# A hybrid decoder stack on one Trainium2 core: attention's value sums completed in memory, rotary latent queries laid out by matrix products

## The chip, the cores and the metric

The kernel runs on one core of one Trainium2 chip. The metric is the device time of one execution in microseconds (us). The engines are named as in the profile: PE (TensorE matmul), PEld (TensorE weight load), DVE (VectorE), ACT (ScalarE), POOL (GpSimd) and SP (SyncE, which issues the DMAs here).

## The reference, cut to what matters

Two post-norm decoder layers on 1024 tokens of width 1024, in float32. In each layer one input projection feeds four mixers side by side, whose outputs are joined and projected; then come a layer norm, a SwiGLU network of inner width 2816, and another layer norm.

```python
y_a = _gmlp_mixer(...)      # chunked spatial gating
y_b = _mla_mixer(...)       # latent attention, 4 heads, 64 plain + 32 rotary columns
y_c = _dilated_mixer(...)   # three dilated windows, 4 heads of 64
y_d = _mlstm_mixer(...)     # chunkwise mLSTM
y = jnp.concatenate([y_a, y_b, y_c, y_d], axis=-1) @ w_out[l]
x = _layer_norm(DEEPNORM_ALPHA * x + y, ln1_g[l], ln1_b[l])
h = (jax.nn.silu(x @ w_gate[l]) * (x @ w_up[l])) @ w_down[l]
x = _layer_norm(DEEPNORM_ALPHA * x + h, ln2_g[l], ln2_b[l])

# latent attention
q = (_rms_norm(c_q) @ w_uq).reshape(..., GROUP_HEADS, 64 + 32)
q = jnp.concatenate([q[..., :64], _rope(q[..., 64:], pos)], -1)
kv = (_rms_norm(c_kv) @ w_ukv).reshape(..., GROUP_HEADS, 64 + 64)
k = jnp.concatenate([k_nope, k_rope broadcast over heads], -1)
o = causal softmax(q k^T / sqrt(96)) v
```

## The kernel before, in words

**Precision.** A float32 product is made of products in the type fp32r. Each operand is split into a high part, a copy in fp32r, and a low part, the difference (`split`, L140 to L146: the copy on ACT, the subtraction on DVE or POOL). `mms` (L121 to L124) issues the chains of matmuls, so most matmuls of the profile bear line L124.

**Order of a layer.** `build` runs the mixers' projections (`mix_a`, `mix_d`, `z_b`, `z_c`), then `attention`, `out_proj`, `ffn1`, `ffn2`. Instructions are placed by a scheduling layer; inside attention the order on PE is instead the order of the program (`manual_schedule`, `MAN`), while the queues of DVE, ACT, POOL and SP are still set by the scheduler.

**Attention** (`attn`, L792). There are four groups of two heads: groups 0 and 1 are the dilated mixer, groups 2 and 3 the latent one. A group has 16 rows, a row being 128 queries of one head; the query blocks come in pairs (`jp` 0 to 3), in the order 0 and 3, then 1 and 2. For a row, `scores` (L798) multiplies queries and keys into PSUM in chunks of 512 keys: two matmuls a chunk, three in the latent groups, where the third takes the rotary part (`QR` and `R`). DVE adds the mask and takes the maximum (L816), ACT makes the exponential (L820), POOL divides by the sum (L823). `turn` transposes the row (tile `pt`, L840) and splits the result into `PH` and `PL`. Two rows later `values` (L849) multiplies by the values (`pv`, L861). Scores run three rows ahead. Between rows PE takes jobs from a list (`fill`), which prepare the next group's operands, so that a job's matmuls stand in PE's queue between those of two rows.

**Sum halves of the values.** The value tile holds the high part in columns 0 to 63 and the low part in 64 to 127, so `pv` has two halves over partitions that must be added. Two ACT copies (L873, L874) bring them to the tile `tmp`, POOL adds them (L875). For groups 0 and 1 the sum goes to memory (`ys`, L877), for 2 and 3 into the tiles `Yb`. Four of the eight value blocks of group 0 have no low part ("full", L871).

**Queries.** `put_q` (L784) makes for each head `q1` (the high part in both halves of the partitions: two ACT copies, L787 and L789) and `q2` (the low part on DVE, L788; the other half set to zero by POOL, L790).

**Rotary part of the latent queries.** For each quarter of the tokens, `rot` multiplies (`prb`), rotates on DVE, and writes each head's 32 columns four times side by side (`qr`, two DVE instructions of 128x512, L1033). `turn` of `b_vqr_jobs` transposes these (`ptr`, eight of 128x128, L1044) and makes `QR`: ACT copies all (L1047), DVE puts the low part over half of it (L1048). In the list of jobs it is `rot`, `vals`, `turn` for each quarter.

**Output projection** (`out_proj`). `prep_w` loads and splits the weights, `ysplit(h)` (L1183) loads the mixers' outputs for one half of the tokens into tiles `yr` and splits them into `yT`; both use the pool `r` of two buffers. Then `proj` multiplies (`po`), half by half.

Of the kernel before, what the change touches and what calls it, by code (L numbers as in the profile page):

```python
# [13 lines left out]
L = 2  # L14
# [4 lines left out]
NT = S // 128  # L19
# [39 lines left out]
class Net:  # L59
# [712 lines left out]
    def qk_tiles(self, pool, pool2=None):  # L772
        f = lambda n, p=pool: self.u(n, F32R, p)
        return [f("kst") for _ in range(2)], [f("q1") for _ in range(2)], [f("q2", p) for p in (pool2 or (pool, pool))]
# [8 lines left out]
    def put_q(self, pq, q1, q2, cols):  # L783
        nc = self.nc  # L784
        for hh in range(2):
            r, o = slice(64 * hh, 64 * hh + 64), slice(64 - 64 * hh, 128 - 64 * hh)
            nc.scalar.copy(q1[hh][r, cols], pq[r, :])  # L787
            nc.vector.tensor_sub(q2[hh][r, cols], pq[r, :], f32(q1[hh][r, cols]))  # L788
            nc.scalar.copy(q1[hh][o, cols], pq[r, :])  # L789
            nc.gpsimd.tensor_scalar(out=q2[hh][o, cols], in0=self.ident[o, 0:1].to_broadcast([64, 512]), scalar1=0.0, scalar2=None, op0=ALU.mult)  # L790

    def attn(self, groups):  # L792
# [57 lines left out]
        def values(n):  # L850
# [5 lines left out]
            pairs = PHL.pop((id(G), jp, hh))  # L856
            m = 64 if full else 128
            for b in range(nb):
                c0 = 128 if b == nb - 1 else 0
                for x, Pt in enumerate(pairs):  # L860
                    nc.tensor.matmul(pv[0:m, c0:256], lhsT=V[2][:, b, hh * 64:(hh + 1) * 64] if full else V[hh][:, b, :], rhs=Pt[b // 4][:, b % 4, c0:256],  # L861
                                     start=b == 0 and x == 0, stop=b == nb - 1 and x == len(pairs) - 1)
            tmp = self.t2("tmp", 512)
            y, spill = tmp[0:64, 0:256], None
            if "Y" in G:
                y = G["Y"][jp // 2][64 * hh:64 * hh + 64, (jp % 2) * 256:(jp % 2) * 256 + 256]
            else:
                l, g = G["spill"]
                spill = self.io["ys"][l, 2, jp // 2, 64 * hh:64 * hh + 64, g * 512 + (jp % 2) * 256:g * 512 + (jp % 2) * 256 + 256]
            if full:  # L870
                nc.scalar.copy(y, pv[0:64, 0:256])  # L871
            else:
# [105 lines left out]
    def b_vqr_jobs(self, ct, w, out):  # L978
# [4 lines left out]
        def rotk(half):  # L983
# [8 lines left out]
            for r in (slice(32, 64), slice(96, 128)):  # L992
                nc.vector.tensor_sub(R[r, cols], pt[r, :], f32(R[r, cols]))
        def start():
            out["V"] = [[self.u("V", F32R if i < 2 else F32, "A").rearrange("p (t n) -> p t n", t=NT) if (any(f) if i == 2 else not all(f)) else None
                         for i in range(3)] for f in FULL[2:]]
            out["QR"] = [[self.u("QR", F32R, "A").rearrange("p (h n) -> p h n", h=2) for _ in range(2)] for _ in range(2)]
        def vals(t2):
# [6 lines left out]
            pv = pv.rearrange("p (t n) -> p t n", t=2)  # L1005
            ts = slice(t2 * 2, t2 * 2 + 2)
            for g in range(2):
                if FULL[2 + g][t2]:
                    nc.scalar.copy(V[g][2][:, ts, :], pv[:, :, g * 128:(g + 1) * 128])
                if all(FULL[2 + g]):  # L1010
                    continue
                for hh in range(2):
                    self.split(V[g][hh][:, ts, 0:64], V[g][hh][:, ts, 64:128], pv[:, :, g * 128 + hh * 64:g * 128 + hh * 64 + 64])
        box = {}

        def rot(t2):
# [700 lines left out]
```

## Time and profile before

| | |
|---|---|
| three runs, median (lowest to highest) | 2463.27 us (2462.56 to 2467.29) |
| the profiled execution, its own time | 2466.75 us |
| its span, first to last instruction | 2465.0 us |
| busy: PE, PEld, DVE, ACT, POOL | 96%, 81%, 68%, 42%, 52% |
| mean granted clock of TensorE | 0.983 of full speed |
| attention of layer 0, of layer 1 (us from the span's start) | 283 to 460, 1514 to 1692 |

The busy shares are means over very different stages. The feed-forward networks hold more than half of the span, and there PE has no gaps to speak of; attention is the stage in which all engines work and PE waits. A wait is put down to the event that came last.

### The profile page before, as it was taken

To read this page: it belongs to the slowest core of one execution; us is meant where nothing else is said; L and a number is where in the kernel's file an instruction comes from. 1 tells how busy PE (TensorE), PEld (TensorE's weight loads), DVE (VectorE), ACT (ScalarE), POOL (GpSimd) and SP (SyncE) were. 2 spreads that over 40 slices of the span, in tenths; PEclk is the share of its full clock that TensorE was granted. 3 is DMA by queue.
4 is the path that set the end of the run, shared out by engine and by line. 5 is a ranking of instruction groups with operands and counts; after the bars stand their busy time and mean duration, and the time that the engine had idled before them with its cause. 6 is when DMAs were issued, how large, how long until landed. Compare 5 with 4: busy or idle time off the path is not lost.

```text
span 2465.0 us, 33578 instructions
## 1 busy us (share of the span) xinstructions
PE 2369.9 (96%) x11820; PEld 1992.5 (81%) x11820; DVE 1664.2 (68%) x2986; ACT 1035.7 (42%) x2102; POOL 1287.5 (52%) x1164
## 2 busy tenths in 40 slices
PE   9999878999999999999999999889999999999997
PEld 9889867787888888788797898778878888887886
DVE  7743687469665564789956436774696665647999
ACT  6322568524332323543333226695243323225442
POOL 2124536665555454776621245366655554547865
PEclk9999999999999999999999999899999999999999
DMA  4111001421332332643221110014213323326431
GB/s 166 53 34 48 18 9 57 172 93 52 129 111 82 118 104 102 257 164 123 99 66 52 35 48 18 8 57 171 94 52 129 111 85 117 108 101 253 166 120 68
DMA packets 83350, 237.37 MB, mean 96 GB/s; under 512 B 10912, under 2 KB 13280, under 8 KB 83184
## 3 DMA queue, kind: packets, MB, share of 16 engines
q1 hardware_dynamic: 83184, 235.24, 27.5%
q8 instruction: 94, 1.54, 0.3%
q14 instruction: 72, 0.59, 0.1%
HBM read 174.88 MB, written 60.33 MB: 95 GB/s over the span
## 4 chain that ended last, share of the span: by engine, by line
PE 79%; DVE 11%; ACT 5%; POOL 3%; issue 2%; DMA 0%; POOLq 0%; DVEq 0%; ACTq 0%; SPq 0%
PE gu L124 32%; PE dn L124 13%; PE po L124 6%; PE zc L124 5%; PE zvo L569 4%; PE zdq L521 3%; PE za L124 3%; PE zb L124 3%; PE sc L124 2%; PE pv L861 2%; DVE P L816 1%; PE pt L840 1%; ACT P L820 1%; DVE T L1347 1%; DVE PL L146 1%
## 5 line engine op out<-in xcount | busy, mean ns | idle before, releaser
L124 PE MATMUL gu<-T,fc 128*128 128x512 f32 x2640 | 631.0, 396 | 9.7 <-ACT fc L1265 8.0
L124 PEld LDWEIGHTS gu<-T,fc 128*128 128x128 f32 x2640 | 498.4, 189 | 130.2 <-ACT fc L1265 10.0
L1266 POOL TENSOR_TENSOR fc<-fw,fc 128x512 fp32r<-128x512 f32 x256 | 365.6, 1433 | 348.4 <-ACT fc L1265 344.1
L124 PE MATMUL dn<-dc,dc 128*128 128x512 f32 x1512 | 355.0, 397 | 4.8 <-DVE dc L1266 4.8
L124 PEld LDWEIGHTS dn<-dc,dc 128*128 128x128 f32 x1512 | 286.4, 190 | 73.1 <-DVE dc L1266 5.7
L1265 ACT CAST fc<-fw 128x512 fp32r<-128x512 f32 x256 | 156.9, 620 | 383.1 <-PE gu L124 211.3
L124 PE MATMUL gu<-B,fc 128*128 128x512 f32 x1056 | 258.9, 395 | 0.0
L146 POOL TENSOR_TENSOR dc<-hr,dc 128x512 fp32r<-128x512 f32 x126 | 195.9, 1570 | 85.8 <-ACT dc L143 75.1
L124 PEld LDWEIGHTS gu<-B,fc 128*128 128x128 f32 x1056 | 198.0, 188 | 46.9
L1396 DVE TENSOR_TENSOR Ra<-Ra,gu 128x512 f32<-128x512 f32 x172 | 117.7, 684 | 126.7 <-PE gu L124 111.5
L823 POOL TENSOR_SCALAR P<-P,rs 128x256 f32<-128x256 f32 (+7 forms) x128 | 99.1, 779 | 125.5 <-DVE rs L822 103.8
L124 PE MATMUL po<-wh,yT 128*128 128x512 f32 x512 | 162.1, 396 | 0.0
L124 PE MATMUL zc<-wh,xT 128*128 128x384 f32 x512 | 134.1, 339 | 0.0
L137 POOL TENSOR_TENSOR wl<-raw,wh 128x768 fp32r<-128x768 f32 (+2 forms) x40 | 81.9, 2052 | 85.5 <-ACT wh L132 84.9
L124 PE MATMUL sc<-kst,q 128*128 128x512 f32 (+3 forms) x384 | 111.8, 388 | 12.9 <-DVE mn L816 12.9
L840 PE MATMUL pt<-ident,P 128*128 128x128 f32 x576 | 93.3, 287 | 23.5 <-DVE PL L146 14.9
L124 PEld LDWEIGHTS po<-wh,yT 128*128 128x128 f32 x512 | 96.2, 188 | 22.2
L143 ACT CAST dc<-hr 128x512 fp32r<-128x512 f32 x126 | 77.6, 621 | 82.6 <-DMA hr<-hs 54.8
L1266 DVE TENSOR_TENSOR dc<-dr,dc 128x512 fp32r<-128x512 f32 x72 | 88.5, 1239 | 33.9 <-ACT dc L1265 33.7
L820 ACT ACTIVATE P<-P,mn 128x256 f32<-128x256 f32 (+7 forms) x128 | 99.5, 779 | 27.7 <-DVE mn L816 25.9
L146 DVE TENSOR_TENSOR PL<-pt,PH 128x512 fp32r<-128x512 f32 (+3 forms) x176 | 95.0, 557 | 20.5 <-ACT PH L143 19.3
L1266 POOL TENSOR_TENSOR fc<-s,fc 128x512 fp32r<-128x512 f32 x44 | 68.3, 1553 | 69.7 <-ACT fc L1265 26.2
(378 smaller groups left out, 5034.7 us busy)
## 6 DMA issues: line engine op xcount, KB each, us to landing
fw<-in_wGU SPq DMA_DIRECT2D x88, 512.0 KB, 4.8
hr<-hs SPq DMA_DIRECT2D x142, 256.0 KB, 2.9
dr<-in_wD SPq DMA_DIRECT2D x44, 512.0 KB, 6.2
hs<-Ra SPq DMA_DIRECT2D x40, 512.0 KB, 2.9
hs<-Rb SPq DMA_DIRECT2D x22, 512.0 KB, 5.5
raw<-in_wO SPq DMA_DIRECT2D x16, 512.0 KB, 3.8
x<-x SPq DMA_DIRECT2D x16, 512.0 KB, 2.6
raw<-in_wC SPq DMA_DIRECT2D x16, 384.0 KB, 3.1
```

Of the source, the lines that this page charges most:

```text
L124: self.nc.tensor.matmul(out, lhsT=a, rhs=b, start=first and j == 0, stop=last and j == n - 1)
L137: (eng or nc.gpsimd).tensor_sub(lo[:, :n], raw[:, :n], f32(hi[:, :n]))
L143: nc.scalar.copy(hi, src)
L146: (lo_eng or nc.vector).tensor_sub(lo, src, f32(hi))
L521: step(lambda: nc.tensor.matmul(pz, lhsT=a, rhs=b_, start=n == 0, stop=n == 23))
L569: nc.tensor.matmul(box["p"], lhsT=a, rhs=b_, start=j == 0, stop=j == 23)
L820: nc.scalar.activation(P[:, 0:nk], P[:, 0:nk], AF.Exp, scale=-1.0, bias=m, accum_out=rs[:, 0:1])
L823: nc.gpsimd.tensor_scalar(out=P[:, 0:nk], in0=P[:, 0:nk], scalar1=rs[:, 1:2], scalar2=1.0, op0=ALU.mult, op1=ALU.mult)
L840: nc.tensor.transpose(pt[:, b * 128:(b + 1) * 128], P[:, (b0 + b) * 128:(b0 + b + 1) * 128], self.ident)
L1265: nc.scalar.copy(dst[:, 0:512], src)
L1266: lo_eng.tensor_sub(dst[:, 512:1024], src, f32(dst[:, 0:512]))
L1396: tt = lambda o, a, b, op: v.tensor_tensor(out=o, in0=a, in1=b, op=op)
```

## The change

It has five parts, each made in both layers.

1. **Values.** In groups 0, 1 and 2 one ACT copy takes both halves of `pv` (128x256), and two DMAs of 64x256 write them to two parts of a new array `yp`; for the blocks without a low part, zeros are written from a constant. In group 3 ACT copies one half and DVE adds the other out of PSUM. `ysplit` loads both parts (two loads more for each half of the tokens) and DVE adds them (three adds of 128x512 for each half). `Yb` is one tile.
2. **Queries.** `q1`'s second half is copied by POOL from the first half, in place of ACT's copy from PSUM. `q2`'s zeros are written once for groups 0 and 1, and groups 2 and 3 use the same `q2` tiles again, so that no zeros are written for them.
3. **Rotary queries.** `rot` writes each head once (`qs`, 128x256). For each half of the tokens there are four transposes, one split into `qh` and `ql`, and for each head two matmuls of 512 columns (`pqr`) with a constant of ones and zeros (`selq`), which put copies and parts in their places; ACT copies the result to `QR`. `R`'s halves change to match.
4. **Values of the latent groups** are split by pairs of token blocks, all four heads at once (128x512).
5. The jobs' order changes with it, and `maskC` is loaded before the first group's preparation.

```diff
     def qk_tiles(self, pool, q2=None):
...
+        if q2 is None:
+            q2 = [f("q2") for _ in range(2)]
+            for hh in range(2):
+                o = slice(64 - 64 * hh, 128 - 64 * hh)
+                self.nc.gpsimd.tensor_scalar(out=q2[hh][o, :], in0=self.mask[o, :], scalar1=0.0, scalar2=None, op0=ALU.mult)
...
             nc.scalar.copy(q1[hh][r, cols], pq[r, :])
             nc.vector.tensor_sub(q2[hh][r, cols], pq[r, :], f32(q1[hh][r, cols]))
-            nc.scalar.copy(q1[hh][o, cols], pq[r, :])
-            nc.gpsimd.tensor_scalar(out=q2[hh][o, cols], in0=self.ident[o, 0:1].to_broadcast([64, 512]), scalar1=0.0, scalar2=None, op0=ALU.mult)
+            nc.gpsimd.tensor_copy(q1[hh][o, cols], f32(q1[hh][r, cols]))
...
-                nc.scalar.copy(tmp[0:64, 0:256], pv[0:64, 0:256])
-                nc.scalar.copy(tmp[0:64, 256:512], pv[64:128, 0:256])
-                nc.gpsimd.tensor_tensor(out=y, in0=tmp[0:64, 0:256], in1=tmp[0:64, 256:512], op=ALU.add)
-            if spill is not None:
-                nc.sync.dma_start(spill, y)
+                y = G["Y"][64 * hh:64 * hh + 64, jp * 256:(jp + 1) * 256]
...
+                    nc.scalar.copy(tmp[0:64, :], pv[0:64, 0:256])
+                    nc.vector.tensor_tensor(out=y, in0=tmp[0:64, :], in1=pv[64:128, 0:256], op=ALU.add)
+                return
+            nc.scalar.copy(tmp[0:m, :], pv[0:m, 0:256])
+            for part in range(2):
+                dst = G["spill"][part][64 * hh:64 * hh + 64, jp * 256:(jp + 1) * 256]
+                nc.sync.dma_start(dst, self.io["c_zero"][:, 0:256] if full and part else tmp[64 * part:64 * part + 64, :])
...
-            qrs = []
-            for j in range(2):
-                qr = self.t2("qr", 512).rearrange("p (h a n) -> p h a n", h=4, a=4)
-                nc.vector.tensor_tensor(out=qr, in0=a[:, j].unsqueeze(2).to_broadcast([128, 4, 4, 32]), in1=b[:, j].unsqueeze(2).to_broadcast([128, 4, 4, 32]), op=ALU.add)
...
+            nc.vector.tensor_tensor(out=qs, in0=a, in1=b, op=ALU.add)
+
+        def turn(half):
...
+            pt = self.psum("ptr", "t")
+            for j in range(4):
+                nc.tensor.transpose(pt[:, j * 128:(j + 1) * 128], box["qs"][:, j * 128:(j + 1) * 128], self.ident)
+            box["Q"] = self.t2("qh", dt=F32R), self.t2("ql", dt=F32R)
+            self.split(*box["Q"], pt)
+
+        def lay(half, h):
+
+            pq = self.psum("pqr", "mm")
+            self.mms(pq, [(box["sel"][:, (2 * h + e) * 128:(2 * h + e + 1) * 128], box["Q"][e]) for e in range(2)])
+            nc.scalar.copy(out["QR"][h // 2][half][:, h % 2, :], pq)
...
-        for t2 in range(4):
-            jobs += [f(rot, t2), f(vals, t2), f(turn, t2)]
-        jobs += [f(rotk, half) for half in range(2)]
+        for half in range(2):
+            jobs += [f(rot, 2 * half), f(vals, 2 * half), f(rot, 2 * half + 1), f(vals, 2 * half + 1), f(rotk, half), f(turn, half)]
+            jobs += [(lambda a, b: lambda: lay(a, b))(half, h) for h in range(4)]
...
+                    for f in range(2 if g == 2 else 1):
+                        raw = self.uw("yr", F32, "r")
...
+                        nc.vector.tensor_tensor(out=y[f], in0=y[f], in1=raw[:, 512:1024], op=ALU.add)
```

Three places show how instructions move. The first is PE in group 1 of layer 0, at the first rotary transposes (`ptr`). Before:

```order
L124 MATMUL pvb_3408<-wk_3321,kvT_2202 128x256
L840 MATMUL pt_3423<-ident,P_3259 128x128 x4
L124 MATMUL sc_3431<-kst_2936,q_448_2938 128x256
L124 MATMUL sc_3431<-kst_2936,q_450_2940 128x256
L1044 MATMUL ptr_3439<-ident,qr_3404 128x128
L1044 MATMUL ptr_3439<-ident,qr_3406 128x128
```

And now:

```order
L845 MATMUL pt_3459<-ident,P_3277 128x128 x2
L124 MATMUL sc_3466<-kst_2934,q_448_2936 128x512
L999 MATMUL ptb_3479<-ident,kr_1873 128x128 x4
L1043 MATMUL ptr_3490<-ident,qs_3400 128x128 x4
L124 MATMUL pqr_3499<-qh_3495,selq_3488 128x512
L124 MATMUL pqr_3499<-ql_3496,selq_3488 128x512
L872 MATMUL pv_3503<-PT_3300,zcv_2274 64x256 x3
```

The transposes now stand behind more work of the rows, and the first laying-out products (`pqr`) directly behind the transposes whose split they read.

The second is POOL at the change from group 1 to group 2 in layer 0 (`q_69*` and `q_7*` are the query tiles of groups 2 and 3, `P` the rows to divide). Before:

```order
L790 TENSOR_SCALAR q_690_3854<-ident 64x512 x2
L823 TENSOR_SCALAR P_3870<-P_3870,rs_3880 128x768
L823 TENSOR_SCALAR P_3910<-P_3910,rs_3916 128x384
L875 TENSOR_TENSOR tmp_3951<-tmp_3951 64x256
L823 TENSOR_SCALAR P_3971<-P_3971,rs_3981 128x640
```

And now:

```order
L795 CAST q_697_3836<-q_697_3836 64x512
L828 TENSOR_SCALAR P_3942<-P_3942,rs_3948 128x512
L828 TENSOR_SCALAR P_3972<-P_3972,rs_3982 128x768
L795 CAST q_698_3837<-q_698_3837 64x512
L828 TENSOR_SCALAR P_4026<-P_4026,rs_4033 128x128
```

The zeros need no product; the copies that stand in their place need ACT's copy of one and are read by the next group's scores, and the last of group 2's stands behind the division of group 1's last row.

The third is POOL at the end of layer 0's attention (`yT` are the subtractions of the split for the output projection). Before:

```order
L823 TENSOR_SCALAR P_5100<-P_5100,rs_5112 128x768
L875 TENSOR_TENSOR Yb_4075<-tmp_5150 64x256
L875 TENSOR_TENSOR Yb_4074<-tmp_5197 64x256
L146 TENSOR_TENSOR yT_5278<-yr_5276,yT_5278 128x512
L146 TENSOR_TENSOR yT_5281<-yr_5276,yT_5281 128x512
```

And now:

```order
L828 TENSOR_SCALAR P_5010<-P_5010,rs_5017 128x512
L828 TENSOR_SCALAR P_5033<-P_5033,rs_5045 128x768
L146 TENSOR_TENSOR yT_5214<-yr_5208,yT_5214 128x512
L146 TENSOR_TENSOR yT_5217<-yr_5211,yT_5217 128x512
```

The additions between the last division and the first subtraction are gone from this queue.

## Rows read from the trace of the kernel before

**Rows 1.** Page, part 1: busy time, share of the span, instructions of each engine.

```profile
PE 2369.9 (96%) x11820; PEld 1992.5 (81%) x11820; DVE 1664.2 (68%) x2986; ACT 1035.7 (42%) x2102; POOL 1287.5 (52%) x1164
```

**Rows 2.** Windows: us, busy of PE, PEld, DVE, ACT, POOL (instructions), clock, DMA, GB/s.

```profile
283.00:308.00 25.00, 19.54 (x122) 16.32 (x123) 19.31 (x53) 21.00 (x46) 16.33 (x18) 0.93 0.04 9
308.00:352.00 44.00, 34.99 (x235) 30.23 (x234) 36.19 (x106) 27.85 (x74) 12.62 (x14) 0.92 0.04 10
352.00:405.00 53.00, 44.16 (x276) 37.58 (x274) 42.87 (x120) 46.22 (x107) 30.94 (x35) 0.97 0.13 39
405.00:460.00 55.00, 48.30 (x338) 42.41 (x337) 39.71 (x128) 47.40 (x115) 38.35 (x42) 1.00 0.19 59
460.00:515.00 55.00, 55.00 (x244) 44.75 (x243) 14.62 (x20) 15.54 (x25) 30.08 (x20) 1.00 0.58 210
1514.00:1692.00 178.00, 152.87 (x960) 130.62 (x961) 137.37 (x400) 141.80 (x338) 97.96 (x107) 0.91 0.11 33
```

**Rows 3.** Waits of PE, attention of layer 0: us in total, times, longest.

```profile
PE sc L124 <- DVE mn L816: 7.7, 11, 2.1
PE ptr L1044 <- DVE qr L1033: 7.2, 6, 3.3
PE pt L840 <- DVE PL L146: 6.8, 9, 1.4
PE pv L861 <- ACT q L789: 2.4, 1, 2.4
```

**Rows 4.** Waits of PE, attention of layer 1.

```profile
PE ptr L1044 <- DVE qr L1033: 5.1, 5, 1.7
```

**Rows 5.** Line L789, both layers: who waited for it (us, times).

```profile
  PE pv L861: 4.8, 2
```

**Rows 6.** Chain that ended last, 355 to 390 us, its shares by line.

```profile
by line: ACT P L820 16.5%; issue 11.2%; ACT q L787 10.0%; ACT PH L143 9.4%; PE pv L861 7.3%; ACT q L789 6.2%; ACT kst L780 5.0%; DVE P L816 4.7%; ACT tmp L874 4.2%; DVE PL L146 3.8%; PE sc L124 3.5%; ACT tmp L873 3.1%; DVE R L993 2.9%; PE p
```

**Rows 7.** Groups by line, attention of layer 0: busy us, mean ns, idle before.

```profile
L790 POOL TENSOR_SCALAR q<-ident 64x512 fp32r<-64x512 f32 x12 | 17.7, 1484 | 0.5
...
L874 ACT COPY tmp<-pv 64x256 f32<-64x256 f32 x27 | 10.0, 369 | 0.3
...
L1048 DVE TENSOR_TENSOR QR<-ptr,QR 64x512 fp32r<-64x512 f32 x8 | 5.4, 692 | 1.1 <-ACT QR L1047 1.0
...
L789 ACT CAST q<-pqb 64x512 fp32r<-64x512 f32 x8 | 4.6, 580 | 0.2
...
L1047 ACT CAST QR<-ptr 128x512 fp32r<-128x512 f32 x8 | 4.5, 590 | 2.8 <-PE ptr L1044 2.6
...
L1027 DVE TENSOR_TENSOR ra<-prb,cs 128x256 f32<-128x256 f32 x4 | 1.7, 419 | 0.1
```

**Rows 8.** Timeline of PE, rotary queries of layer 0: start, us, instruction, [wait].

```profile
328.71 0.30 PE L1044 MATMUL ptr<-ident,qr 128*128 128x128 f32 x1 [3.28 <-DVE qr L1033]
329.22 1.76 PE L1044 MATMUL ptr<-ident,qr 128*128 128x128 f32 x7 [0.21 <-DVE qr L1033]
...
338.42 1.04 PE L1044 MATMUL ptr<-ident,qr 128*128 128x128 f32 x8
```

**Rows 9.** Chain that ended last, pieces in order of time: start, us, what.

```profile
462.50 48.13 PE po L124 x207
...
1760.17 1.31 PE ptx L1216 x12
```

**Rows 10.** Tile yT, 400 to 520 us: ns min/median/max, first and last start.

```profile
L146 POOL TENSOR_TENSOR yT<-yr,yT x12: 1280/1294/1746, 434.9 to 483.5; 128x512 fp32r<-128x512 f32 x12
...
L146 DVE TENSOR_TENSOR yT<-Yb,yT x4: 692/736/1587, 434.7 to 469.0; 128x512 fp32r<-128x512 f32 x4
```

**Rows 11.** Groups by line and form, attention of layer 0: row division on POOL.

```profile
L823 POOL TENSOR_SCALAR P<-P,rs 128x512 f32<-128x512 f32 x8 | 5.5, 693 | 3.3 <-DVE rs L822 2.5 <-PE pt L840 0.6
```

**Rows 12.** DMA issues, 455 to 500 us: KB each, median us to landing.

```profile
yr<-ys SPq DMA_DIRECT2D x3, 512.0 KB, 8.2
```

**Rows 13.** Timeline of SP, 395 to 600 us.

```profile
479.61 12.39 SPq L129 DMA_DIRECT2D raw<-in_wO  x4
```

More of the change, by code (lines that the diff above doesn't have):

```diff
@@ L767, in z_c, with qk_tiles @@
         return out, jobs
[L772 to L774 removed]
+    def qk_tiles(self, pool, q2=None):
+        f = lambda n: self.u(n, F32R, pool)
+        kst, q1 = [f("kst") for _ in range(2)], [f("q1") for _ in range(2)]
+        if q2 is None:
[3 more added lines that the diff above has]
+                self.nc.gpsimd.tensor_scalar(out=q2[hh][o, :], in0=self.mask[o, :], scalar1=0.0, scalar2=None, op0=ALU.mult)
+        return kst, q1, q2
     def put_k(self, pk, kst, cols):
@@ L856, in values @@
             pairs = PHL.pop((id(G), jp, hh))
+            if "heads" in G:
+                v = lambda b: V[b // 2][:, b % 2, G["heads"] + hh, :]
+            elif full:
+                v = lambda b: V[2][:, b, hh * 64:(hh + 1) * 64]
+            else:
+                v = lambda b: V[hh][:, b, :]
             m = 64 if full else 128
@@ L991, in rotk @@
             nc.scalar.copy(R[:, cols], pt)
-            for r in (slice(32, 64), slice(96, 128)):
-                nc.vector.tensor_sub(R[r, cols], pt[r, :], f32(R[r, cols]))
+            nc.vector.tensor_sub(R[64:128, cols], pt[64:128, :], f32(R[64:128, cols]))
         def start():
-            out["V"] = [[self.u("V", F32R if i < 2 else F32, "A").rearrange("p (t n) -> p t n", t=NT) if (any(f) if i == 2 else not all(f)) else None
-                         for i in range(3)] for f in FULL[2:]]
-            out["QR"] = [[self.u("QR", F32R, "A").rearrange("p (h n) -> p h n", h=2) for _ in range(2)] for _ in range(2)]
+            out["V"] = [self.u("V", F32R, "A").rearrange("p (t h n) -> p t h n", t=2, h=4) for _ in range(4)]
+            out["QR"] = [[self.u("QR", F32R, p).rearrange("p (h n) -> p h n", h=2) for p in two] for two in ("EB", "AA")]
         def vals(t2):
@@ L1004, in vals @@
                 self.mms(pv[:, j * 256:(j + 1) * 256], [(KV[0][:, ts], wk[0][:, 256:512]), (KV[0][:, ts], wk[1][:, 256:512]), (KV[1][:, ts], wk[0][:, 256:512])])
[L1005 to L1013, printed above, removed]
+            self.split(V[t2][:, :, :, 0:64], V[t2][:, :, :, 64:128], pv.rearrange("p (t h n) -> p t h n", t=2, h=4))
         box = {}
@@ L1037, in turn @@
-        def turn(t2):
-            half, jj = t2 // 2, t2 % 2
-            qrs = box.pop(t2)
-            for gg in range(2):
-                pt = self.psum("ptr", "t")
-                for hh in range(2):
-                    for j in range(2):
-                        nc.tensor.transpose(pt[:, hh * 256 + j * 128:hh * 256 + (j + 1) * 128], qrs[j][:, gg * 2 + hh, :, :].rearrange("p a n -> p (a n)"), self.ident)
-                dst = out["QR"][gg][half][:, :, jj * 256:(jj + 1) * 256]
-                src = pt.rearrange("p (h n) -> p h n", h=2)
-                nc.scalar.copy(dst, src)
-                nc.vector.tensor_sub(dst[64:128], src[64:128], f32(dst[64:128]))
+            if t2 % 2 == 0:
+                box["qs"] = self.t2("qs")
@@ L1675, in layouts @@
     o["c_ident"] = np.eye(128, dtype=np.float32)
+    selq = np.zeros((128, 4, 2, 4, 32), np.float32)
+    for h in range(4):
+        for b in range(4):
+            selq[h * 32 + np.arange(32), h, b % 2, b, np.arange(32)] = 1.0
+    o["c_selq"] = selq.reshape(128, 1024)
+    o["c_zero"] = np.zeros((64, 1024), np.float32)
     sel = np.zeros((128, 8), np.float32)
```

60 lines of the change are left out of this document (31 added, 29 removed).

## The prediction

> **What bounds the kernel now.** I read the page's busy times first, then the windows of the stages that the change touches, then who PE waits for in them, and last the groups that fall away. On the page PE is busy for 2369.9 us of 2465.0 [rows 1], so all that can be gained by better timing is about 95 us, spread over the whole program. The windows say where it lies. PE is idle for 5.5, 9.0, 8.8 and 6.7 us in the four stages of layer 0's attention, together 30.0, and for 25.1 us in layer 1's; where the projection starts it is busy for 55.00 of 55.00 us [rows 2]. The change works only in attention and at the start of the projection, so 55 us is the ceiling of what its timing can bring; the rest must come from PE's own work.
>
> Each stage has its own second engine. In stage 1 (end of group 0) ACT is busy for 21.0 of 25 us, in stage 2 (group 1 with the rotary jobs) DVE for 36.2 of 44, in stage 3 (group 1's end and group 2, with the next queries as jobs) ACT for 46.2 of 53, in stage 4 (groups 2 and 3, no jobs) ACT for 47.4 of 55 [rows 2]. The waits show how this reaches PE: for DVE's maxima 7.7 us, for the rotated queries `qr` 7.2, for the low parts `PL` 6.8, and one wait of 2.4 us that ends with ACT's second copy of a query, the very instruction that the change removes [rows 3]. Layer 1 shows the same: 5.1 us for `qr` [rows 4], and over both layers 4.8 us for that copy [rows 5]. All `qr` waits lie in stage 2 and the copy's in stage 3; of the chain between 355 and 390 us more than half is ACT's [rows 6].
>
> **The change part by part,** in us over both layers, against the profiled execution of 2466.75, which is 3.5 above the median of the runs, 2463.27.
>
> *Rotary queries.* The transposes no longer wait for a `qr` issued just ahead: 7.2 and 5.1 us go [rows 3, 4]. Two waits come. The new transposes wait for `qs`, but with a second group of `prb` products, a row's transposes and its scores in between; between nothing and the 1.7 us of the longest such wait in layer 1 [rows 4], I take 0.5 a layer. And the first `pqr` product stands right behind the transposes whose split it reads: at least one ACT copy of 0.59 and one DVE subtraction of 0.69 [rows 7], so 1.3, and at most the 3.3 of the longest `qr` wait [rows 3, 8]. I take the middle, 2.3; in the second half of the tokens the value products of a row stand in between, and I take nothing. PE's own work: 24 transposes fewer a layer at 1.31/12 = 0.109, so 2.6 less; 16 products of 512 columns more at 48.13/207 = 0.233 [rows 9], so 3.7 more. Sum: -12.3 + 5.6 + 2 x 1.1 = **-4.5** (between -7.5 and -0.1). DVE loses more here (eight subtractions of 0.69 become two, and the `qr` writes are halved), but stage 2's PE waits that are named hang on `qr` alone, so I count no more for it.
>
> *ACT in stage 3.* Eight query copies of 0.58 and about a third of the 27 second value copies of 0.37 go [rows 7], 7.9 us of ACT's 46.2, and its chain is the one that PE waits for. The wait of 2.4 us on the copy goes; of the other 6.4 us of idle time I take ACT's relief in proportion, 17%, so 1.1. That is 3.5 a layer, **-7.0** (nothing if DVE, busy for 42.9 of 53, takes over at once; at most the stage's idle time, 17).
>
> *Stage 1.* Four copies of 0.58 and some four of 0.37 leave ACT's 21.0; 18% of 5.5 us is 1.0 a layer, **-2.0** (0 to -10).
>
> *Stage 4.* ACT loses 8 x 0.37, and POOL its additions. But DVE gets eight additions out of PSUM (0.42 each by the nearest form, 128x256 [rows 7]) and, near the end, three additions of sum halves at about 0.74, the median of DVE's `yT` subtractions of the same size [rows 10]: 5.6 us on 39.7. With ACT the busier engine but `PL` and the maxima, both DVE's, the waits, I take 14% of 6.7 us as a loss: **+1.9** (-3 to +5).
>
> The same row shows how uncertain those additions are: that subtraction, with both inputs in SBUF, took 1587 ns at most where its median is 736, while POOL was subtracting too [rows 10]. The Trainium skill (SBUF — State Buffer, Who interferes with whom) says that a DVE instruction with two SBUF inputs and a GpSimd instruction that reads SBUF block each other for a whole instruction; by that rule each of the three could wait a POOL subtraction of 1.29 us longer, which by the same proportion would make the sum 1.3 us worse. The row's maximum fits the rule, its median says that it seldom strikes, so the sum goes by the median.
>
> *Query copies on POOL.* The zeros (64x512, 1.48 us each [rows 7]) go from the latent groups; a copy comes for each, of some 0.7 us by the nearest contiguous form, 128x512 at 0.69 [rows 11], and 1.48 at most. POOL has room (30.9 of 53), but group 2's last copy stands behind the division of group 1's last row, and the third score of the new group reads it; the last query products also move a row later. Below nothing is excluded, since this copy only adds a step; above I put the 2.4 that PE loses there today. I take 1 a layer: **+2.0** (0 to 4.8).
>
> *Clock.* After the longest `qr` wait, seven transposes took 1.76 us where eight took 1.04 without one [rows 8]: TensorE had fallen to the lower of its levels (1.2 for 2.4 GHz), and a batch then costs 0.85 more. Fewer such waits save some of it: **-1.0** (0 to -5).
>
> *Projection.* Both split loads and the 96 spill DMAs (32 before) are covered by PE's unbroken work there [rows 2]; nothing is charged. If that cover fails it is the last rival below. `maskC`, the merged splits of the values and of `R` only relieve DVE and ACT further and are counted at nothing.
>
> **Sum:** -4.5 - 7.0 - 2.0 + 1.9 + 2.0 - 1.0 = **-10.6 us**. Against the profiled execution that is 2456.2, against the median **2452.7**.
>
> **The rivals.** *(a) New waits eat the gain.* The direct `ptr`-`pqr` step costs 3.3 in each half of the tokens rather than 2.3 once (+8.6 over both layers), and DVE takes over in stage 3 (half of the 7.0 is lost). Then the sum is +1.5, no change: 2464.8. For it: DVE's load of 81% in stage 3 does not fall. Against it: in stage 2 DVE is relieved of a good part of its 36 us, and its queue is what makes such waits long.
>
> *(b) The relief spreads.* In a chain over three engines each about 80% busy, waits fall faster than loads. If half of the 55.1 us of idle time in attention goes, the time is 2463.3 - 27.5 = 2435.7. For it: stages 1 to 3 lose 8 to 20% of ACT's or DVE's work at once. Against it: stage 4 has a quarter of the idle time and gains nothing on DVE.
>
> *(c) Slower: the sum halves come late.* The projection's tiles pass two buffers. Two loads more for each half of the tokens are one turn more of both: a load at 8.2 us to landing when the queues are full [rows 12], an addition of 0.7 to 1.6 and a subtraction of 1.3 [rows 10], so some 11 us a half. The last weights, today issued between 479.6 and 492 us [rows 13], are behind them. PE reaches them after both halves of four tokens, 2 x 4 x 24 x 0.233 = 45 us behind 462.5 [rows 9], at some 507. That is 15 us behind their last issue, of which landing, copy and subtraction take about half, so the case decides once they come 7 us later than now. If POOL's relief (its subtractions today start only behind the last value addition, which leaves its queue) makes up for one of the two turns, 11 us of lateness remain and a layer loses 4; if for neither, 22 remain and it loses 15. That is 2461 or 2483; the middle is 2472. Against it speaks that relief, and that PE's work there has no gap today.
>
> **How the numbers follow.** A difference of 0.2%, 4.9 us, is about what a measurement of this kernel can tell from none. My forecast, 2444 to 2458, gets 0.50; (b), 2430 to 2444, 0.20; (a), 2458 to 2468, 0.19; (c), 2468 to 2480, 0.11. So faster by over 0.2% is 0.70, within it 0.19, slower 0.11. The range is 2435 to 2465: it leaves out (c), the far end of (b) and the last of (a), about 2 in 10.
>
> **What would show it.** If the steps are right, PE's list of waits has no `ptr` behind DVE above 1 us a layer, a new entry `pqr` behind DVE's `ql` of 1.3 to 3.3 us, none of 2.4 us behind ACT's query copy; ACT is busy for about 38 us in stage 3, DVE for some 45 in stage 4; attention is 4 to 7 us shorter in each layer, and PE is unbroken for 50 us behind it. I am wrong if stage 3 stays as long with ACT relieved, if scores at the start of group 2 wait for POOL's copy by more than 2.4 us, or if `po` products wait for `yT` or `wl`.

## The result and the profile after

| | before | after |
|---|---|---|
| median (lowest to highest), us | 2463.81 (2462.56 to 2467.29) | 2436.36 (2432.69 to 2440.11) |
| the profiled execution, its span | 2466.75, 2465.0 | 2433.93, 2432.2 |

The ratio is 0.9888, 95% interval 0.9873 to 0.9902. The gain is **27.45 us** where 10.6 was forecast. The time lies in the range and on the right side, but it is that of rival (b). The page of the changed kernel, part 1, beside [rows 1]:

```profile
PE 2352.3 (97%) x11804; PEld 1975.9 (81%) x11804; DVE 1651.0 (68%) x2966; ACT 993.6 (41%) x1996; POOL 1239.9 (51%) x1116
```

**Equal stretches of work.** The stages of [rows 2] have other times now, so I cut both traces where the same work begins: at the first `pv` product of a pair of rows, a value block, 32 in each attention. *Stretch 1* runs from the 1st to the 6th, *2* to the 12th (the rotary jobs), *3* to the 18th (the query jobs), *4* to the 32nd. The windows view, columns as in [rows 2], of the kernel before, stretches 2 and 3 of both layers, and the sum over all eight:

```profile
311.33:361.21 49.88, 38.97 (x260) 33.95 (x260) 42.39 (x118) 32.49 (x85) 15.69 (x19) 0.93 0.04 9
361.21:398.43 37.22, 30.68 (x186) 26.21 (x185) 29.28 (x80) 33.35 (x76) 23.52 (x24) 0.95 0.18 54
...
1541.65:1594.14 52.49, 43.90 (x260) 37.93 (x260) 42.30 (x120) 32.59 (x85) 15.61 (x19) 0.80 0.04 9
1594.14:1630.26 36.12, 30.61 (x186) 26.16 (x185) 28.98 (x78) 33.62 (x77) 23.57 (x25) 0.95 0.09 26
...
sum 348.27, PE 294.97 PEld 253.23 DVE 267.44 ACT 276.68 POOL 190.96; mean PE 36.87 PEld 31.65 DVE 33.43 ACT 34.59 POOL 23.87
```

And of the changed kernel:

```profile
312.74:352.87 40.13, 36.35 (x247) 31.55 (x247) 30.23 (x92) 29.20 (x68) 9.64 (x13) 0.96 0.12 30
352.87:384.63 31.76, 29.86 (x191) 25.59 (x190) 29.84 (x81) 27.48 (x65) 12.61 (x19) 1.00 0.16 43
...
1526.94:1565.45 38.51, 34.74 (x248) 30.81 (x248) 30.24 (x92) 29.18 (x68) 9.62 (x13) 1.00 0.13 32
1565.45:1597.23 31.78, 29.85 (x191) 25.64 (x190) 29.87 (x81) 27.46 (x65) 12.63 (x19) 1.00 0.16 42
...
sum 307.92, PE 279.67 PEld 241.44 DVE 254.98 ACT 242.08 POOL 129.55; mean PE 34.96 PEld 30.18 DVE 31.87 ACT 30.26 POOL 16.19
```

The eight stretches are 40.4 us shorter. PE's idle time (length less busy) falls from 53.3 to 28.3, which is 25.0, and its busy time by 15.3. Stretch 2 gives 23.7 (9.75 and 13.98), stretch 3 9.8. The two spans differ by 32.8 us, so some 7.6 us are lost again elsewhere (below). The two profiled executions are not the medians: the one before lies 2.9 us above its median, the one after 2.4 below, so the traces show 5.4 us more of a gain than the medians do.

PE's waits in layer 0's attention, beside [rows 3]:

```profile
PE pt L845 <- DVE PL L146: 4.1, 6, 1.0
PE sc L124 <- DVE mn L821: 2.6, 8, 0.7
PE pt L845 <- POOL P L828: 2.3, 2, 1.8
PE pv L872 <- DVE q L794: 1.6, 2, 1.2
...
PE ptr L1043 <- DVE PL L146: 1.2, 1, 1.2
PE ptr L1043 <- DVE qs L1032: 1.1, 1, 1.1
PE pqr L124 <- ACT qh L143: 0.7, 1, 0.7
PE pqr L124 <- DVE ql L146: 0.6, 1, 0.6
```

The waits for `qr` and for ACT's query copy are gone. The new ones around `ptr` and `pqr` come to 3.6 (the same in layer 1), and the wait for the maxima fell from 7.7 to 2.6 though nothing was done to the maxima.

**Where time was lost.** The start of the rows, from the first score to the first value block, took 15.35 and 14.34 us before and takes 18.03 and 18.47 now. These two windows of the changed kernel, and POOL's timeline in the first:

```profile
272.86:290.89 18.03, 13.76 (x76) 11.85 (x75) 12.79 (x42) 10.14 (x26) 13.18 (x15) 0.91 0.00 0
1488.20:1506.67 18.47, 13.70 (x75) 11.81 (x73) 12.97 (x42) 10.28 (x25) 13.32 (x16) 0.91 0.00 1
```

```profile
274.21 5.61 POOL L779 TENSOR_SCALAR q<-maskC 64x1024 fp32r<-64x1024 f32 x2 [0.68 <-PE zc L124]
```

Group 1's zeros are now one block of 5.6 us just where POOL has the first rows to divide; PE's list above has `pt <- POOL P` with 2.3 us, 1.8 the longest. And from the first `po` to the first product of the next network (`gu`) it takes 96.7 and 96.8 us, before 95.3 and 95.2. DVE's timeline in that stretch, after and then before:

```profile
499.44 0.69 DVE L1279 TENSOR_TENSOR s<-fw 128x512 f32<-128x512 f32 x1 [7.75 <-DMA fw<-in_wGU]
```

```profile
508.46 0.69 DVE L1269 TENSOR_TENSOR s<-fw 128x512 f32<-128x512 f32 x1 [2.65 <-DMA fw<-in_wGU]
```

DVE, which also has the layer norm to do, now waits 7.75 us for the next network's weights, whose loads stand in SP's queue (489.0 us) behind those of the sum halves (461.2). PE's wait for these weights' copies grows from 4.0 to 6.2, the same in layer 1. Before and after:

```profile
PE gu L124 <- ACT fc L1265: 4.0, 1, 4.0
```

```profile
PE gu L124 <- ACT fc L1275: 6.2, 1, 6.2
```

### The profile page after: what moved, and what is told of

Read it like the earlier page. It is cut to its first block, busy times and chain, and to the rows that moved or that the text cites. A ratio compares the mean times of both kernels' runs of the same rounds, so it can differ in the third digit from the quotient of the medians.

```text
span 2432.2 us, 33480 instructions
## 1 busy us (share of the span) xinstructions
PE 2352.3 (97%) x11804; PEld 1975.9 (81%) x11804; DVE 1651.0 (68%) x2966; ACT 993.6 (41%) x1996; POOL 1239.9 (51%) x1116
## 4 chain that ended last, share of the span: by engine, by line
PE 75%; DVE 10%; POOL 5%; DMA 3%; issue 3%; ACT 3%; SPq 0%; POOLq 0%; DVEq 0%; ACTq 0%
PE gu L124 34%; PE dn L124 13%; PE zc L124 5%; PE zvo L569 4%; PE zdq L521 3%; PE za L124 3%; PE zb L124 3%; PE pv L872 2%; PE sc L124 2%; PE pt L845 2%; DVE P L821 1%; DMA yr<-yp 1%; DVE ma L1505 1%; PE po L124 1%; POOL ma L1135 1%
## 5 line engine op out<-in xcount | busy, mean ns | idle before, releaser
L124 PE MATMUL gu<-T,fc 128*128 128x512 f32 x2640 | 630.3, 396 | 13.7 <-ACT fc L1275 12.3
L124 PEld LDWEIGHTS po<-wh,yT 128*128 128x128 f32 x512 | 95.8, 188 | 23.2 <-DVE x L1215 1.5
L146 DVE TENSOR_TENSOR PL<-pt,PH 128x512 fp32r<-128x512 f32 (+3 forms) x176 | 95.2, 557 | 16.3 <-ACT PH L143 15.6
```

The costliest lines, as they stand in the source:

```text
L124: self.nc.tensor.matmul(out, lhsT=a, rhs=b, start=first and j == 0, stop=last and j == n - 1)
L146: (lo_eng or nc.vector).tensor_sub(lo, src, f32(hi))
```

## The experiments

All were timed against the kernel before on the same chip, in three series (its medians 2463.77, 2464.22 and 2464.86). *Gain* is the distance to that median. The changed kernel's 27.45 comes from a series of its own. By the intervals each gain can be off by some 3 us to either side (4 for e6), so a difference of two gains says something from about 5 us on. In every run the scheduler also sets the queues of DVE, ACT and POOL anew, so that an edit moves more than its own instructions. The windows come from one profiled execution of each kernel.

| run | what | median, us | gain | ratio, 95% interval |
|---|---|---|---|---|
| e1 | before + rotary part | 2447.40 | 16.4 | 0.9917 to 0.9943 |
| e2 | before + value sums | 2461.59 | 2.2 | 0.9983 to 1.0 |
| e3 | before + queries | 2453.52 | 10.3 | 0.9943 to 0.9967 |
| e4 | before + values by pairs | 2452.68 | 11.1 | 0.9942 to 0.9969 |
| e5 | before + filling transposes | 2455.28 | 8.9 | 0.9955 to 0.9979 |
| e6 | change less rotary part | 2449.98 | 14.2 | 0.9937 to 0.997 |
| e7 | change less pairs | 2440.25 | 24.0 | 0.9891 to 0.9916 |
| e8 | change, both mends | 2418.06 | 46.2 | 0.9806 to 0.9831 |
| e9 | change less queries | 2450.45 | 14.4 | 0.9929 to 0.9954 |
| e10 | change less value sums | 2443.70 | 21.2 | 0.9904 to 0.9931 |
| e11 | change, zeros early | 2431.33 | 33.5 | 0.9853 to 0.988 |
| e12 | change, small tiles | 2428.88 | 36.0 | 0.9843 to 0.987 |

**One part alone (e1 to e4).** Each edit is a part of the diff ahead of the prediction, made in the kernel before; its core is shown. e1:

```diff
-        for t2 in range(4):
-            jobs += [f(rot, t2), f(vals, t2), f(turn, t2)]
...
+            jobs += [f(rot, 2 * half), f(vals, 2 * half), f(rot, 2 * half + 1), f(vals, 2 * half + 1), f(rotk, half), f(turn, half)]
+            jobs += [(lambda a, b: lambda: lay(a, b))(half, h) for h in range(4)]
```

> The kernel before with the rotary part of the change alone (qs, selq, the split qh/ql, the laying-out products, the merged subtraction of R, and the job order). Theory 1, the rotary waits carry the gain: with the waits for qr gone TensorE keeps its upper clock in the rotary stretch of both layers, so this part alone gives 15 to 22 us of the 27.5, nearly all of it between the sixth and the tenth value block of each attention. Theory 2, the relief spreads: every part takes some load off ACT, DVE or POOL and none carries it alone; this part gives 6 to 12 us. Theory 3, the prediction's own sum: 4 to 5 us. By all three the start of the attention rows and the projection stay where they were (within 1 us).

e2:

```diff
-                nc.gpsimd.tensor_tensor(out=y, in0=tmp[0:64, 0:256], in1=tmp[0:64, 256:512], op=ALU.add)
...
+            nc.scalar.copy(tmp[0:m, :], pv[0:m, 0:256])
```

> The kernel before with the change of the value sums alone (one ACT copy, two halves to memory, DVE adds them ahead of the projection; group 3 added by DVE out of PSUM). Theory 1: 0 to 4 us faster, since the rotary waits remain, and 6 to 7 us of that is lost again in the two projections, so within 4 us of the kernel before on either side. Theory 2: 5 to 10 us faster in the attention stages, less the same loss. Theory 3 (the prediction's sum): about 3 us faster, no loss in the projection. All expect the first ptx about 3 us later behind the first po than in the kernel before, if the lateness of the loads is this part's.

e3:

```diff
-            nc.scalar.copy(q1[hh][o, cols], pq[r, :])
...
+            nc.gpsimd.tensor_copy(q1[hh][o, cols], f32(q1[hh][r, cols]))
```

> The kernel before with the change of the queries alone (POOL copies the second half, zeros written once for groups 0 and 1, mask loaded early). Theory 1: 0 to 3 us faster; the two zero writes of 64x1024 on POOL make the first value block of each attention 2 to 4 us later, as in the changed kernel. Theory 2: 4 to 8 us faster. Theory 3: 0 to 2 us faster, no lateness at the start.

e4:

```diff
-                for hh in range(2):
-                    self.split(V[g][hh][:, ts, 0:64], V[g][hh][:, ts, 64:128], pv[:, :, g * 128 + hh * 64:g * 128 + hh * 64 + 64])
+            self.split(V[t2][:, :, :, 0:64], V[t2][:, :, :, 64:128], pv.rearrange("p (t h n) -> p t h n", t=2, h=4))
```

> The kernel before with the splits of the latent values by pairs of token blocks alone. The prediction counted this part at nothing. Theory 1: up to 2 us faster. Theory 2: 3 to 6 us faster, because eight small instructions per quarter become two on ACT and DVE in the stretch where DVE is the busiest second engine. Theory 3: no difference.

Windows of e1, stretches 2 and 3 of both layers:

```profile
310.52:352.04 41.52, 37.84 (x248) 32.60 (x247) 31.11 (x103) 31.78 (x85) 12.70 (x16) 0.92 0.08 23
352.04:391.07 39.03, 32.19 (x191) 28.64 (x190) 30.27 (x81) 34.41 (x78) 24.98 (x26) 0.91 0.16 50
...
1533.34:1571.63 38.29, 34.81 (x248) 30.89 (x248) 31.02 (x103) 31.41 (x85) 12.70 (x16) 1.00 0.09 25
1571.63:1612.04 40.41, 32.36 (x191) 28.20 (x190) 30.22 (x81) 34.46 (x78) 25.02 (x26) 0.92 0.08 23
```

Of e3, stretch 3 of both layers:

```profile
360.04:391.80 31.76, 29.10 (x187) 24.74 (x185) 29.09 (x80) 28.85 (x68) 16.63 (x24) 1.00 0.18 51
...
1586.24:1618.08 31.84, 28.96 (x186) 24.72 (x185) 28.65 (x78) 28.98 (x68) 16.67 (x24) 1.00 0.10 30
```

Of e4, stretch 2 of both layers:

```profile
310.86:357.12 46.26, 37.05 (x260) 31.50 (x260) 41.11 (x108) 31.38 (x73) 15.95 (x18) 1.00 0.04 10
...
1532.58:1579.50 46.92, 38.27 (x260) 32.79 (x260) 41.11 (x108) 31.56 (x73) 15.87 (x18) 0.96 0.04 9
```

The rotary part alone shortens stretch 2 by 8.4 and 14.2 us, to the length that it has in the changed kernel within 1.4, and makes stretch 3 longer by 1.8 and 4.3. The queries alone bring stretch 3 to the 31.8 of the changed kernel, and bring the late start too (18.7 and 18.5 us from first score to value block). The pairs, counted at nothing, shorten stretch 2 by 3.6 and 5.6. The value sums alone shorten stretch 3 by 2.5 and 1.4 and bring the lateness of the projection (96.8 and 96.5 us). e1 came out as theory 1 said and e2 within its bounds (its 2.2 us are not told from none); e3 and e4 gave more than any theory had expected. The four gains add up to 40, more than the whole. One reason is in layer 1's stretch 2: before, it ran at a mean clock of 0.80, and every one of the four kernels runs it at 0.90 or more, so that the same time is won four times. That 0.80 is of one execution, whose mean clock of 0.983 is a low one: in the 38 that the three series timed it went from 0.982 (2468.70 us) to 0.989 (2459.54 us).

**Waits filled (e5).**

```diff
                 pt = self.psum("ptr", "t")
+                if gg == 0:
+                    for _ in range(10):
+                        nc.tensor.transpose(pt[:, 0:128], self.ident, self.ident)
```

> The kernel before with ten extra 128x128 transposes of the identity ahead of every first rotary transpose (40 a layer; they write the same bank and are overwritten, so the computed values stay). Nothing is relieved; TensorE only stays at work for some 1.1 us of each wait for qr. Theory C, part of the changed kernel's gain is the clock alone: in layer 1 TensorE stays at 2.4 GHz between the sixth and the twelfth value block, that stretch falls from 52.5 to 45 to 48 us, the whole by 4 to 8 us. Rival theory W, the waits are all: the stretch stays, and the whole is the same or up to 4 us slower.

Windows of stretch 2, both layers:

```profile
311.02:357.81 46.79, 40.44 (x300) 35.77 (x300) 41.59 (x118) 32.09 (x85) 14.90 (x19) 1.00 0.04 10
...
1535.20:1581.94 46.74, 40.38 (x300) 35.71 (x300) 41.50 (x118) 32.18 (x85) 14.81 (x19) 1.00 0.04 9
```

With 40 matmuls more, stretch 2 is 3.1 and 5.8 us shorter, and the kernel 8.9 us faster. TensorE stays at 2.4 GHz, where before it had fallen to 1.2 in between. The scheduler also moved some of DVE's and ACT's instructions in this stretch, among them two `qr` writes of 128x512 that stand earlier now, so the edit is not the clock alone. But the waits did not shrink by it: idle time fell by 6.8 us over both layers, and the 80 added transposes take an estimated 8.7 (at 0.109 each, the price of [rows 9]). What fell is the time of the same 260 matmuls, by some 10.8 us in the sum of both layers by the same estimate. So the clock is worth about 9 us in the kernel before without any relief. Theory C holds; its upper figure was even a little low.

**One part less (e6, e7, e9, e10).** The edits are the same four parts, each taken back in the changed kernel.

> The changed kernel without its rotary part (qr written four times, transposed and split as in the kernel before; all other parts kept). Theory S, each stage has one limit which one part removes: the rotary stretch (sixth to twelfth value block; 40.1 and 38.5 us in the changed kernel, 49.9 and 52.5 before) goes back to 45 to 50 us in both layers and the whole loses 12 to 20 us of the 27.5. Theory D, the relief is shared by all parts: the stretch goes back by a third to a half, the whole loses 6 to 11 us. The stretch behind it stays at 31 to 33 us by theory S.

> The changed kernel with the latent values split head by head as in the kernel before. Alone this part gave 11 us. Theory S: beside the rotary part it has nothing left to give in the rotary stretch, so the whole loses 0 to 3 us. Theory D: it loses 4 to 9 us.

> The changed kernel with the queries made as before (ACT copies the second half from PSUM, POOL writes 64x512 zeros for every half of all groups). Theory S, each stage has one limit which one part removes: the stretch of the query jobs (twelfth to eighteenth value block; 31.8 us in the changed kernel, 37.2 and 36.1 before) goes back to 35 to 40 us, although the value sums still spare ACT a copy there; the start of the rows (first score to first value block, 18.0 and 18.5 us) goes back to 14 to 16. Both together: 2 to 8 us slower than the changed kernel's 2436.4. The prediction's step (ACT's relief shortens that stage in proportion, the copy on POOL costs 1 us a layer): 1 us slower or less, the stretch at 33 us.

> The changed kernel with the value sums as before (two ACT copies, POOL adds, one spill; Yb for groups 2 and 3). Theory S: the stretch of the query jobs stays below 34 us, the one behind it (eighteenth to last value block, 61.8 us) grows by 1 to 3 us a layer, and first po to critical part of the next stage shrinks by 1.5 us a layer (first po to first gu 95.3 again rather than 96.7): together within 4 us of the changed kernel on either side. The prediction's steps (ACT's relief in stage 3 is a third this part's, DVE loses 1 a layer): 2 us slower.

Stretch 3 of both layers without the queries:

```profile
350.82:389.05 38.23, 32.33 (x192) 28.48 (x191) 29.92 (x80) 32.28 (x73) 20.05 (x19) 0.91 0.14 36
...
1572.96:1610.74 37.78, 32.35 (x192) 28.45 (x190) 29.84 (x80) 32.18 (x73) 20.06 (x19) 0.91 0.13 35
```

And without the value sums:

```profile
352.23:387.42 35.19, 29.85 (x192) 25.76 (x191) 29.97 (x82) 29.76 (x71) 17.83 (x26) 1.00 0.17 51
...
1569.12:1604.71 35.59, 30.88 (x192) 27.08 (x190) 29.52 (x80) 29.58 (x70) 17.81 (x26) 0.95 0.10 26
```

Within the whole, the rotary part is worth 27.45 - 14.2 = 13.2 us, the queries 13.0, the value sums 6.3, the pairs 3.5. Without the rotary part, stretch 2 is 47.6 and 45.3 us long, as theory S has it:

```profile
311.68:359.23 47.55, 38.37 (x261) 32.17 (x261) 40.95 (x106) 29.68 (x68) 12.23 (x13) 0.96 0.06 15
...
1533.30:1578.61 45.31, 36.76 (x261) 31.47 (x260) 40.91 (x106) 29.61 (x68) 11.33 (x13) 1.00 0.07 16
```

The clock stays up there although the waits for `qr` are back: of the 14.2 us by which stretch 2 is longer than in the changed kernel, 10.2 are idle time. Without the queries, stretch 3 is longer than it was before the change, at a clock of 0.91. There the theory was too simple, and the total, 2 to 8 us expected, is a miss: beside the rotary part, which pushes five matmuls into stretch 3, both the query copies and the value sums are needed to keep it short. e10 missed too: stretch 3 grew by 3.4 and 3.8 us where it was to stay, stretch 4 did not grow (61.57 and 62.17); only the projection behaved as expected (95.2 us from first `po` to first `gu` in both layers). The pairs are nearly used up by the rotary part (11.1 alone, 3.5 with it); the two intervals do not tell 3 from 4, the border of the theories.

How an ACT copy reaches PE is seen in the kernel before, on ACT, DVE and PE in stretch 3:

```profile
364.89 0.58 ACT L789 CAST q<-pqb 64x512 fp32r<-64x512 f32 x1
365.48 0.58 ACT L787 CAST q<-pqb 64x512 fp32r<-64x512 f32 x1
```

```profile
366.17 0.69 DVE L788 TENSOR_TENSOR q<-pqb,q 64x512 fp32r<-64x512 f32 x1 [0.57 <-ACT q L787]
366.89 0.69 DVE L816 CUSTOM_DVE_ANT_0 P<-sc,maskC 128x512 f32<-128x512 f32 x1
```

```profile
367.64 0.73 PE L124 MATMUL sc<-kst,q 128*128 128x512 f32 x2 [2.07 <-DVE mn L816]
```

The second copy of one head (L789) stands ahead of the other head's first copy (L787); DVE waits for that one to subtract, the row's maximum waits in DVE's queue behind the subtraction, and PE waits for the maximum. The wait is booked on `mn`, but it begins two queues further up, with ACT. Of the 2.07 us this chain puts 0.58 down to the copy L789. In e3 PE does not wait at this place at all: the copy is gone, and the scheduler has also set the maximum (363.20 us) ahead of the subtraction (364.53) in DVE's queue. The runs do not part the two.

**The two losses mended (e8, e11, e12).** In e11 both groups' `q2` are made and zeroed ahead of the first group's preparation; in e12 the sum halves are loaded into tiles of the pool `t2`, from which the rows take `tmp` too; e8 has both.

```diff
+        for g in (0, 1):
+            G[g]["q2"] = self.q2_tiles("A")
         for f in self.prep_c_jobs(zc[0], G[0]):
...
-                        raw = self.uw("yr", F32, "r")
-                        nc.sync.dma_start(raw[:, 0:1024].rearrange("p (a n) -> p a n", a=2),
...
+                        parts = [self.t2("yr") for _ in range(2)]
+                        for a in range(2):
+                            nc.sync.dma_start(parts[a], io["yp"][l, f if g == 2 else 2][a, :, h * 512:h * 512 + 512])
```

> The changed kernel with two places mended: the zeros of both latent-free groups are written ahead of the first group's preparation (group 1's two POOL writes of 64x1024 today stand among the first rows), and the sum halves are loaded into idle small tiles instead of the two shared buffers of the projection's loads. If the two POOL writes hold up the first rows, the first value block comes 2 to 4 us earlier in each layer, of which 0 to 3 are left at the sixth block. If the loads in the shared buffers delay the weights, the first ptx comes 3 us earlier behind the first po in each layer. Then 2426 to 2433; if neither holds, within 2 us of the changed kernel's 2436.

> The changed kernel with group 1's zeros written ahead of the first group's preparation, nothing else. First score to first value block falls from 18.0 and 18.5 to 15 to 16 us; the whole is 4 to 9 us faster than the changed kernel, if the start is what most of the 18 us of the double mend came from; the projection stays (first po to first gu 96.7).

> The changed kernel with the sum halves loaded into idle small tiles, nothing else. First po to first gu falls from 96.7 to 95 to 96 us and the first wait of the next network for its weights' copies by 2 us a layer; the whole is 5 to 9 us faster than the changed kernel. The start of the rows stays (18.0 and 18.5).

First score to first value block in e8, both layers:

```profile
272.90:288.25 15.35, 12.56 (x75) 10.45 (x73) 11.88 (x41) 10.99 (x27) 10.79 (x16) 1.00 0.00 1
1480.80:1496.16 15.36, 12.60 (x75) 10.46 (x73) 11.90 (x41) 11.02 (x27) 10.76 (x16) 1.00 0.00 1
```

Stretch 4 of both layers in e12 (61.78 and 61.84 in the changed kernel), and PE's wait for the next network's weights in layer 0:

```profile
384.96:443.79 58.83, 53.90 (x383) 48.11 (x382) 46.28 (x149) 46.38 (x113) 31.89 (x33) 1.00 0.32 98
...
1596.82:1655.57 58.75, 53.83 (x382) 48.22 (x382) 46.40 (x150) 46.41 (x113) 31.96 (x33) 1.00 0.32 98
```

```profile
PE gu L124 <- ACT fc L1275: 4.0, 1, 4.0
```

The zeros cost 6.1 us (33.5 - 27.45), the way the sum halves are loaded 8.5. Both came out as expected in the whole (first score to first value block was 16.6 us in e11, a little above; first `po` to first `gu` fell to 95.8 and 95.9 in e12). But stretch 4, which no one expected to move, is 3 us shorter a layer in e12, and that is not the buffers' lateness. For its first 40 us PE's work in it runs as in the changed kernel, within 0.15 us; then these stand in the changed kernel's DVE queue, and PE waits behind the first:

```profile
424.03 1.17 DVE L146 TENSOR_TENSOR yT<-yr,yT 128x512 fp32r<-128x512 f32 x1
427.59 0.69 DVE L1199 TENSOR_TENSOR yr<-yr 128x512 f32<-128x512 f32 x1
```

```profile
425.95 1.17 PE L845 MATMUL pt<-ident,P 128*128 128x128 f32 x8 [0.81 <-DVE PL L146]
```

In e12 the same transposes do not wait, because the loads of the halves are issued at 440.1 us rather than at 417.9, and the first addition runs behind the stretch:

```profile
425.32 1.03 PE L845 MATMUL pt<-ident,P 128*128 128x128 f32 x8
```

```profile
446.07 0.69 DVE L1199 TENSOR_TENSOR yr<-yr,yr 128x512 f32<-128x512 f32 x1
```

By the stretch's end PE is 2.4 us ahead in both layers; the other 0.6 to 0.7 are three `po` products that have left it. So e12 undoes two losses at once: three additions and a subtraction that delay the rows' own work on DVE (2.4 us a layer), and the late loads (0.9 us a layer to the first `gu`, 2.2 in its wait for weights). Together the mends give 18.7, four more than their sum and more than was expected of e8. The intervals do not tell four from none, and in the traces 5.5 of a surplus of 5.9 us lie behind the first `gu` of each layer, where the mends change nothing but the place of the zeros. **e8, 2418.06 us, is faster than both kernels**, by 46.2 and by some 18 us.

## Why the prediction was right and wrong

**Right:** what bounds PE, that the `qr` waits and the copy's wait go, and the loads of the second engines. In the stage that [rows 2] call 3 (345.8 to 391.2 us now) ACT is busy for 38.25 us where 38 was said, in stage 4 (391.2 to 445.3) DVE for 44.54 where 45 was said. The new waits around `ptr` and `pqr` are 3.6 a layer, forecast 2.8; that in front of `pqr` is 1.3, the low end of the forecast. Two of the signs named fail: `ptr` still waits for DVE by 2.3 us a layer where 1 was the limit, and attention, from the first score to the first `po`, is 14.5 and 19.0 us shorter where 4 to 7 was said.

**Wrong, by terms.** Two steps failed above all: that the clock is worth 1 us, and that stage 2's waits hang on `qr` alone. Work and clock together were to make PE's busy time 1.2 us longer (2 x 1.1 - 1.0); in the eight stretches it fell by 15.3. The waits were to fall by 11.8 (the sum less these 1.2); idle time fell by 25.0.

- *Rotary queries, -4.5.* The part gives 16.4 alone and 13.2 within the whole. The balance of the waits that I could name was about right (12.3 gone, 7.2 come). But I counted nothing else, on the ground that the named waits hung on `qr` alone. In e1, idle time in stretch 2 falls from 10.9 and 8.6 to 3.7 and 3.5 us, 12.3 net: behind the shorter DVE queue PE's waits for `PL` (3.9 over both layers), `QR` (1.5) and `R` (1.6) go too, and 7.0 of new ones come.
- *Clock, -1.0.* In proportion this is the term furthest off. The 260 matmuls of stretch 2 are busy for 37.05 us at a clock of 1.00 (e4, layer 0); before, the same 260 were busy for 38.97 and 43.90, so the lower level cost 8.8 us in this stretch alone, in the execution that was profiled. By their granted clocks, 0.983 and 0.991, TensorE stood at the lower level for an estimated 84 us of the profiled execution before and 44 of the one after. I had priced it from a single batch of transposes in layer 0, and did not look at the clock of layer 1's stretch, though [rows 2] give 0.91 for the whole of its attention. In the changed kernel that stretch runs at 1.00. The Trainium skill (TensorE: Matmul & The Clock Gate, HAM oscillation — how this bites in real kernels) describes a kernel that waits for a DMA after each group of matmuls and begins the next at the lower level every time, and advises a loop order that keeps TensorE busy. Here the waits are for DVE, and not every one is followed by the lower level (in e4, layer 0, six waits for `qr` of 1.6 us at most passed at a clock of 1.00); e5 agrees with the advice, with 8.9 us for added work.
- *Values by pairs, 0.* 16 subtractions of 0.29 and 16 copies of 0.27 us a layer became four of 0.68 and four of 0.58. I counted a relief of DVE by 1.9 us a layer as nothing in the stretch where DVE is the busiest second engine; alone it is worth 11.1. But in stretch 2 that is nearly all clock: of the 9.2 us that e4 saves there, 7.6 are busy time of the same 260 matmuls and 1.6 idle time.
- *ACT in stage 3, -7.0, and query copies on POOL, +2.0.* The net of -5 stands against 9.8 in stretch 3. e3 alone brings 9.7. Relief in proportion to load missed how the copies stand in the chain to the maxima, where DVE's subtraction waits for ACT and the maximum for the subtraction. The copy on POOL takes 0.608 us and PE waits for none.
- *The zeros.* The step said that they go from the latent groups and priced those that go. It did not follow those that stay: in group 1, two of 2.77 us, moved to the head of its jobs. This cost 6.1 us, and turned *Stage 1, -2.0* into a loss: from the first score to the sixth value block it is 1.6 and 1.1 us longer, where in e11 it is 2.0 and 1.4 shorter.
- *Stage 4, +1.9.* Stretch 4 is 0.9 and 1.8 shorter, so the relief was worth more than was charged. The loss on DVE is there all the same: against e12, the halves' additions and their subtraction cost 2.4 us a layer. The additions in SBUF took 0.69 us in the median and 1.73 at most, beside a subtraction on POOL; the Trainium skill's rule (SBUF — State Buffer, Who interferes with whom) fits the maximum; of the twelve additions it lengthened one.
- *Projection, 0.* Rival (c)'s mechanism is there: loads behind two shared buffers come late. PE's own list shows no `po` waiting for `yT` or `wl`, which is what I had asked of it; the lateness passes through DVE's queue to the layer norm and the next network. In e12 DVE's wait for that network's weights falls from 7.75 to 1.36 us, and the lateness that goes is some 3 us a layer; the 8.5 us of e12 hold the loss in stretch 4 too.

**The rivals.** (b), half of the idle time, is what came: 25 of 53 us. That its time was met is in good part luck: its reason, that waits fall faster than loads, gives the 25, but 15.3 us of busy time came on top, which it did not have, and the losses at the start and in the projection, with the 5.4 us between the profiled executions and the medians, took about as much away. (a) is refuted: the step to `pqr` costs 1.3 us once a layer, not 3.3 twice, and stretch 3 is shorter although DVE's load there stayed. (c)'s lateness is real, some 3 us a layer where its lower price was 4, but it is paid in the next network, not in front of `po`, and lies under the larger gain.

**Left open:** from the first `gu` to the next layer's first score it took 949.7 us and takes 947.1, and from layer 1's first `gu` to the end 678.0 and 678.5, though each holds 2.2 us more of the wait for weights. So some 6 us of the profiled difference come from work that the change hardly touches, about what the two executions differ from their medians. In the fourteen traces the first of these pieces takes from 944.4 to 949.9 us. I assign them to no part.

## What to carry to other kernels

A wait is booked on the last event, but its cause can be two queues further up: follow it there before pricing a relief by an engine's load. Cut both traces at the same piece of work, layer by layer, and read the clock of each piece before summing; where it is below 1.00, the price of a wait is the wait and the slow matmuls behind it. Of what a change moves, price what stays as well as what goes, at its new place in its queue, and ask of every new load whose buffer it takes, and between whose work its follow-up on DVE will stand.

## What the runs showed of the hardware that I had not expected

Forty extra transposes a layer, put where TensorE waits, made the kernel 8.9 us faster: in layer 1's stretch 2 the granted clock rose from 0.80 to 1.00, and PE was busy for 40.38 us with 300 matmuls where it had been busy for 43.90 with 260. The single waits in that stretch before were short, 1.7 us at most [rows 4]. And the clock differs between executions of one program: in 38 of the kernel before it went from 0.982 to 0.989, and the two times at these ends lie 9 us apart.
